# Neighbourhood layer: the low parts of all weights are made on VectorE, none on GpSimd

## The chip, the cores and the metric

The kernel runs on one core of a Trainium2 chip. The metric is the device time of one execution in microseconds (us), the median of three timed runs. Instructions run on five engines, which the trace calls PE (TensorE, with PEld for its weight loads), DVE (VectorE), ACT (ScalarE), POOL (GpSimd) and SP (SyncE, which here issues the DMAs).

## The reference, cut to what matters

Two layers of a diffusion backbone on 512 latent tokens (a grid of 8 rows by 64 columns) and 256 context tokens, 1024 features each. A layer normalises and modulates the tokens, projects them, mixes them, gates the result and projects it back. Layer 0 mixes with differential attention, layer 1 (the layer of the change) with attention over a neighbourhood on the grid, plus all context tokens:

```
def neighbourhood_mixer(u_lat, u_ctx, w_in, w_out, ...):
    q, k, v, z = jnp.split(u @ w_in, 4, axis=-1)      # latent and context tokens
    q = rms_norm(q per head of 64); k = rms_norm(k per head of 64)
    s     = q . k over an 8 x 16 window * scale + relative bias
    s_ctx = q . k_context * scale
    p     = softmax(concatenate([s, s_ctx]))
    o     = p_band . v_band + p_ctx . v_context
    return (o * silu(z)) @ w_out
```

All is float32. Layer 1 has 32 heads of 64 features; `w_in` is 1024 x 8192.

## The kernel before, in words

**Arithmetic.** The tensor engine takes operands in a reduced float32 format (float32r). To keep the accuracy, each operand x is held as two tiles: a high part, hi = float32r(x), and a low part, lo = x - hi. A product is three matmuls: hi hi, hi lo and lo hi (`project`, line 505). For weights, `split_w` (line 480) makes both: one DMA brings a raw tile `wraw` of two blocks of 128x512, ScalarE casts each block into `whi`, and then an engine subtracts, `wlo = wraw - whi`. That engine is VectorE unless the caller passes another.

**Loops.** Layer 1 runs over 16 groups of two heads. In the loop over groups (method `run`), step g does the attention of group g and, in the same ten half steps, the projections of group g + 1, as work that TensorE can do in between. The weights of a group come in four parts, q0 to q3, of two blocks each (eight blocks are the 1024 features in tiles of 128). `loads` (line 498) asks in step g for q0 at half step 6, q1 and q2 at half step 9, all for group g + 2, and for q3 at half step 0 for group g + 1. The tuple `POOL_B` names the parts whose low tiles are made by GpSimd: (0, 2), so q0 and q2; those of q1 and q3 are made by VectorE. That holds for groups 2 to 15; the weights of groups 0 and 1 are asked for outside `loads`, and their low parts are VectorE's. Layer 0 has the same scheme with `POOL_A`, which is empty: in its groups VectorE makes all low parts, apart from those of group 0.

**Buffers.** There are two `wraw` buffers, eleven `whi` and eleven `wlo` (`BUFS`, line 34). A raw buffer is free for the next DMA when both low tiles of its part are made. A `whi`/`wlo` buffer is free when TensorE has used its weights for the last of the six tiles of 128 tokens that a group projects.

**Other work on these engines.** In a group VectorE also normalises q and k (`qd`, `kk`), splits the transposed queries and keys (`qT`, `KSb`), the values (`Vb`) and the transposed softmax weights (`wTb`), adds the bias (`Sb`) and joins halves (`pair`). GpSimd finishes 1/rms (`ssk`, `rsk`) and multiplies by the gate (`yb`).

**Order.** Nothing is issued where it is noted. The class `Plan` (lines 131 to 277) notes every instruction and simulates a run: an engine takes, among the instructions that are ready at that moment, the one that was noted first. The order in which the simulated run starts them is the order in each engine's queue, which the chip then follows strictly. The simulation takes a price for each instruction (`Op.estimate`, line 94), among them

```
if e == "DVE": ...  return n / 0.96 + (129 if len(reads) > 2 else 69)     # ns; 602 for 128x512
if e == "POOL": ... return n * 0.83 + 36 if name == "memset" else n * 2.1 + 150   # 1225 for 128x512
```

It has no term for one engine's work slowing another's. In the profile all instructions carry line 277, where the plan issues them, so they are told apart by tiles.

Of the kernel before, what the change touches and what calls it, by code (L numbers as in the profile page):

```python
# [15 lines left out]
PSUM = bass.MemoryType.PSUM  # L16
DRAM = bass.MemoryType.DRAM
# [8 lines left out]
# token halves of 256: 0 = context, 1 and 2 = latent  # L26
# [10 lines left out]
# half steps of a projection between the parts of the attention  # L37
LAG = dict(pw=2.5, pv=1.5, po=0.5, py=1.5, qka=2, qkb=3, b1=2, b2=1.5, b3=1, bo=0.5, by=3)
# half steps at which the weights of the next groups are loaded, and the scores of a head begin
AT = dict(a0=8, a1=11, a2=11, a3=0, b0=6, b1=9, b2=9, b3=0, s0=5, s1=7, c0=2, c1=7, sa=0, cg=2, ch=9, c2=9, cv=1)  # L40
# half steps of the last group that begin an output projection
FILL_A, FILL_B = (0, 1, 2, 3, 5, 7, 9, 11, 13, 15, 16, 17), (2, 4, 6, 8, 10, 11, 12, 13)
START_DVE = (0,)
# parts of the first modulation that the tensor engine takes in float32
# [9 lines left out]
POOL_A, POOL_B = (), (0, 2)  # L54


class Pool:
    """tiles of a pool by tag, with the number of buffers of each tag in one place"""
# [12 lines left out]
# ns from the end of an instruction to the start of one that needs it  # L71
# [12 lines left out]
class Op:  # L84
    """an instruction that waits for its place: its engine, what it touches, what it is likely to take"""
# [8 lines left out]
    def estimate(self, name):  # L94
        """ns"""
        out, reads, e = self.writes[0], self.reads, self.engine
        n = math.prod(out.shape[1:])
        psum = any(x.space == PSUM for x in [out] + reads)
        if e == "PE":
            return 2.5 + n * (1 if reads[0].dtype == F32R else 2 if name == "transpose" else 4) / 2.4 if n > 2 else 260  # L100
        if e == "ACT":
            return n / 1.2 + (51 if psum else 93) + 93 * (len(self.writes) - 1 + name.startswith("act") * (len(reads) - 1))
        if e == "DVE":
            if name == "tensor_reduce":
                return math.prod(reads[0].shape[1:]) / 0.96 + 66
            if name in ("tensor_scalar", "tensor_copy", "memset") and not psum:
                return n / 1.92 + 69 + 60 * (len(reads) - 1)
            return n / 0.96 + (129 if len(reads) > 2 else 69)
        if e == "POOL":
            if any(x == ALU.pow for x in self.args):  # L110
                return 300 + 165 * n
            return n * 0.83 + 36 if name == "memset" else n * 2.1 + 150
        return max(56, math.prod(out.shape) / 90)


class Rec:
    """an engine that notes its instructions"""
# [13 lines left out]
class Plan:  # L131
    """notes the program, then issues every engine's instructions in the order of a simulated run"""
# [6 lines left out]
    def touching(self, tiles):  # L139
        """what has been noted so far that touches one of these"""  # L140
        names = {t.name for t in tiles}
        return {i for i, op in enumerate(self.ops) if any(x.name in names for x in op.writes + op.reads)}

    @staticmethod
    def region(x):
        """of a tile: partitions and columns, or all of it in PSUM; of memory in DRAM: the range"""
        dims = list(x.ap)
        if x.space == DRAM:
            return 0, 1, x.offset, x.offset + sum(s * (n - 1) for s, n in dims) + 1
        lo = x.offset % math.prod(x.tensor.shape[1:])  # L150
        hi = lo + 1 + sum(s * (n - 1) for s, n in dims[1:] if s > 0)
        lo += sum(s * (n - 1) for s, n in dims[1:] if s < 0)
        if x.space == PSUM:
            return 0, P, 0, 1
        p = x.start_partition
        p = p() if callable(p) else p
        return p, p + dims[0][1], lo, hi

    def depend(self):
        """what each instruction has to come after"""  # L160
        seen = {}
        for i, op in enumerate(self.ops):
            op.after = set(op.behind)
            at = [(x, self.region(x), w) for w, xs in ((True, op.writes), (False, op.reads)) for x in xs]
            for x, r, w in at:
                # two engines do not read a tile in PSUM at a time
# [14 lines left out]
    def order(self):  # L181
# [4 lines left out]
        place, count = {}, {}  # L186
# [16 lines left out]
        def offer(i):  # L203
            """to its engine, unless a buffer is missing"""
# [18 lines left out]
        out = []  # L223
        while len(out) < len(ops):
# [11 lines left out]
            # two of a tag at once, or a buffer gone since  # L236
# [4 lines left out]
            if e == "PE":  # L241
                # the tensor engine's clock is halved after an idle window
# [37 lines left out]
class K:  # L280
# [3 lines left out]
    # ------------------------------------------------------------ constants  # L284
# [19 lines left out]
    def load_vecs(self):  # L304
        """silu of both conditioning vectors, on every partition"""
# [23 lines left out]
    def mod_first(self):  # L329
        """scale and shift of layer 0 on the tensor engine; two steps per two tiles of features"""  # L330
# [7 lines left out]
        # columns: hi of both vectors, lo of both; their sums are the products with the weights' hi and lo  # L338
# [53 lines left out]
    def first_u(self, x, v, u, n, half):  # L392
        """two tiles of features of u hi / lo from x / rms"""
# [12 lines left out]
    def scaled(self, x, s, half):  # L406
        """x / rms, in place"""
        for n in range(4):
            eng = self.nc.gpsimd if 4 * half + n in X_POOL else self.nc.vector
            eng.tensor_tensor(x[n], x[n], s.unsqueeze(1).broadcast_to([P, 2, 256]), ALU.mult)  # L410

    def mod_chunk(self, layer, ch):
        """e[:, ch] = (W^T chunk) . silu(c) for both vectors"""
# [9 lines left out]
    def mod_finish(self, layer, v, part):  # L423
        """part 0: shift b, 1: a = g (1 + scale), 2: gate"""
# [8 lines left out]
    # ------------------------------------------------------------ modulated norm  # L433
    def norm_stats(self, x, tag="qd", on_pool=False):
        """x: four [128, 2, 256] (feature-major) -> 1 / rms, on every partition"""
# [9 lines left out]
        # a token to a partition for the power, then to every partition  # L445
# [14 lines left out]
    def make_u(self, x, s, a, b):  # L460
        """x, 1 / rms -> u hi / lo"""
# [17 lines left out]
    # ------------------------------------------------------------ weights  # L479
    def split_w(self, src, n, shape, eng=None, tag="wraw"):  # L480
        """n blocks of weights in one load, hi and lo each"""
# [16 lines left out]
    def loads(self, Wn, W, layer, g, hs, on_pool):  # L498
        """weights of the next groups: the last part of g + 1 and the others of g + 2"""
# [5 lines left out]
    def project(self, o, W, u, j, kts, c=slice(0, 512)):  # L505
        """one tile of 128 tokens (tile j of a half) x the columns of a group"""
# [10 lines left out]
    # ------------------------------------------------------------ order of work: half steps  # L517
# [3 lines left out]
    def tick(self, step=0.5):  # L521
        """everything that is due by now"""
# [9 lines left out]
    def drained(self, gen, fill, hs):  # L532
        """what is left of the attention, with the steps of other work for the half steps that follow"""
# [7 lines left out]
    # ------------------------------------------------------------ per-head rms of q and k  # L541
# [5 lines left out]
    def rstd(self, sq):  # L547
        """squares [128, 2, 128] -> 1 / rms of each 64 columns, [128, 4]"""
# [8 lines left out]
    def put_q(self, t, rs, dst):  # L557
        """t [128, 128] (two heads) times rs, each head twice, into dst [128, 2, 2, 64]"""
# [9 lines left out]
    def q_transposed(self, qds):  # L568
        """two tiles [128, 2, 2, 64] -> [128, head, hi / lo, 256]"""
# [15 lines left out]
    def k_transposed(self, ks, KS, half):  # L585
        """two tiles [128, 128] -> stacks of hi and lo; head 0: (hi; lo), head 1: (lo; hi)"""
# [16 lines left out]
    def gained(self, out, x, g):  # L603
        """[128, 2, 128] times a gain [128, 2, 64] of both heads"""
# [3 lines left out]
    def rope(self, ps, t):  # L608
        """(q | k) of a latent tile, rotated and times the norm's gains"""
# [14 lines left out]
    # ------------------------------------------------------------ layer 0: differential attention  # L624
    def a_tables(self):
# [16 lines left out]
        # (1 - lam_init) * gain of the sub-layer norm, with the half of the gate's silu  # L642
        nc.sync.dma_start(self.subg, A["subg"].broadcast_to([P, P]))
        nc.vector.tensor_scalar(self.subg, self.subg, 0.5 * (1.0 - LAM_INIT) * math.sqrt(P), None, ALU.mult)
        # -lambda
# [15 lines left out]
    def a_tile(self, G, half, j, ps):  # L661
        """queries, keys, values and gate of a tile of 128 tokens"""
# [37 lines left out]
    def a_scores(self, g, G, half, j):  # L700
        """scores of 128 queries with both heads' keys, softmax and difference of the two"""
# [20 lines left out]
        # l0 (p0 / l0 - lambda p1 / l1); the norm that follows takes l0 out again  # L722
# [67 lines left out]
    # ------------------------------------------------------------ layer 1: neighbourhood attention  # L790
    def b_tables(self):
# [3 lines left out]
        # the scores come out negated: q's gain carries the sign  # L795
# [12 lines left out]
    def b_project(self, G, U, W):  # L808
# [3 lines left out]
        for half in range(3):  # L812
            V = sb.tile([P, 2, 4, 64], F32R, name="Vb", tag="V")
            G["v"][half] = V
            if half == 0:
                # keys and values alone: both tiles share a bank
# [44 lines left out]
    def b_v_hi(self, ps, V):  # L861
        """values [.., 128] -> [.., 4, 64]: head 0: hi | lo, head 1: lo | hi"""
# [6 lines left out]
    def b_bias(self, g, h):  # L869
        """minus the bias, and what masks: one per place of a query block in the row; the last part is for the context"""  # L870
# [43 lines left out]
    def b_weights(self, pn, kts):  # L914
        """transposed weights of the key tiles asked for: 0..3 latent, 4 and 5 context"""
# [33 lines left out]
    def b_third(self, g, G, h, o, w):  # L949
        nc, pair = self.nc, G["pair"]  # L950
        self.b_values(G, h, o, w)
        # the halves of the products with the values' hi and lo
# [7 lines left out]
    def b_gate(self, g, G):  # L960
        nc, sb = self.nc, self.sb
        # silu carries a half
# [24 lines left out]
    # ------------------------------------------------------------ output projection  # L987
    def keep(self, layer, g, py, c):
        """what the last group leaves goes straight to an output projection that has begun"""
# [8 lines left out]
    def out_proj(self, layer, halves, gates, places, xtag, xs, late=None):  # L998
        """h + gate * (y @ w_out) of the tokens of one half or two; a step per 128 features, and one for the first loads;
        late: buffers for the rest of y, the last part first, for a second round"""  # L1000
# [77 lines left out]
    # ------------------------------------------------------------ everything  # L1078
# [168 lines left out]
def _host(inp):  # L1247
# [9 lines left out]
    # a head's 64 features as (half of the rotation, axis, frequency)  # L1257
# [31 lines left out]
    # relative bias: query p = (column, row), key (column offset, row)  # L1289
# [53 lines left out]
```

## Time and profile before

| | |
|---|---|
| time, median of 3 runs | 1829.35 us (1828.93 to 1829.58) |
| span of the profiled execution, first to last instruction | 1827.4 us |
| PE busy | 1775.6 us (97% of the span) |
| PEld busy | 1509.2 us (83%) |
| DVE busy | 1487.5 us (81%) |
| ACT busy | 969.8 us (53%) |
| POOL busy | 602.2 us (33%) |
| chain that ended last | PE 75%, DVE 15%, ACT 5% |

The span is what the trace shows of one execution; its own time on the clock of the timed runs is not recorded separately, and the median of those runs is 1.95 us above the span. The groups of layer 0 run from about 75 to 780 us and the groups of layer 1 from about 1050 us to 1690 us; output projections follow each.

A matmul's duration overlaps the next one's: 128x512 matmuls of 0.39 us start every 0.23 us. So PE counts as idle only where no matmul runs at all. Where a row of the timeline joins several instructions (x2, x3), its duration is from the first start to the last end.

### The profile page before, as it was taken

Reading aid. Unit: us, or ns where it says so; the run is one execution under the profiler, and the core shown is the slowest. Engines: PE = TensorE matmul, PEld = TensorE weight load, DVE = VectorE, ACT = ScalarE, POOL = GpSimd, SP = SyncE. Lnnn points to the kernel's source line nnn. Section 1 sums busy time; section 2 is a strip of 40 time slices with the busy share of each in tenths; the row PEclk is TensorE's granted clock in tenths of the full one; section 3 lists DMA queues with packets and bytes.
Section 4 is the critical chain, followed back from the end, with each engine's and each line's share of the span. In section 5 each row is a group of like instructions: output and inputs, shape, how many; then the busy total and the mean of one; then the engine's idle time right before and its main releaser. Section 6 shows DMA issues by size and latency. Waiting matters only on the chain.

```text
span 1827.4 us, 29430 instructions
## 1 busy us (share of the span) xinstructions
PE 1775.6 (97%) x10032; PEld 1509.2 (83%) x10032; DVE 1487.5 (81%) x3437; ACT 969.8 (53%) x2654; POOL 602.2 (33%) x915
## 2 busy tenths in 40 slices
PE   7899999999999999999999999999999999999999
PEld 3688888888888888888889988888888888888887
DVE  5888999898999999989858777777777777777863
ACT  4456555555555555556636455555555555555641
POOL 4544434444444444343100123333333333332100
PEclk9899999999999999999999999999999999999999
DMA  7401222121222222223556321111122211111423
GB/s 282 136 15 56 76 79 67 56 71 59 65 78 87 79 79 76 78 72 105 187 156 215 100 78 62 61 61 61 63 70 68 67 61 61 61 61 61 146 95 104
DMA packets 60774, 160.74 MB, mean 88 GB/s; under 512 B 7376, under 2 KB 22096, under 8 KB 59728
## 3 DMA queue, kind: packets, MB, share of 16 engines
q1 hardware_dynamic: 60624, 158.86, 26.7%
q8 instruction: 79, 1.29, 0.3%
q14 instruction: 71, 0.58, 0.1%
HBM read 144.68 MB, written 14.16 MB: 87 GB/s over the span
## 4 chain that ended last, share of the span: by engine, by line
PE 75%; DVE 15%; ACT 5%; issue 2%; POOL 2%; DMA 0%; SPq 0%; DVEq 0%; ACTq 0%; POOLq 0%
PE pj L277 40%; PE pjo L277 12%; PE oT L277 4%; PE S L277 4%; PE Sb L277 3%; PE pwb L277 3%; ACT pexp L277 3%; DVE wlo L277 3%; POOL ms L277 2%; PE pq L277 2%; DVE nm L277 2%; PE pw L277 1%; PE oTb L277 1%; DVE kk L277 1%; DVE t L277 1%
## 5 line engine op out<-in xcount | busy, mean ns | idle before, releaser
L277 PE MATMUL pj<-whi,ufirst 128*128 128x512 f32 x1536 | 524.6, 402 | 2.4 <-ACT ufirst L277 1.9
L277 PEld LDWEIGHTS pj<-whi,ufirst 128*128 128x128 f32 x1536 | 289.9, 189 | 58.1 <-ACT ufirst L277 2.5
L277 PE MATMUL pj<-wlo,ufirst 128*128 128x512 f32 x768 | 303.2, 395 | 0.0
L277 PE MATMUL pj<-wlo,uhi 128*128 128x512 f32 (+1 forms) x768 | 278.5, 363 | 12.1 <-DVE wlo L277 12.1
L277 PE MATMUL pj<-whi,uhi 128*128 128x512 f32 (+1 forms) x768 | 279.5, 364 | 0.0
L277 PE MATMUL pj<-whi,ulo 128*128 128x512 f32 (+1 forms) x768 | 276.3, 360 | 0.0
L277 ACT CAST whi<-wraw 128x512 fp32r<-128x512 f32 x352 | 209.3, 631 | 105.1 <-PE pjo L277 31.5
L277 DVE TENSOR_TENSOR wlo<-wraw,whi 128x512 fp32r<-128x512 f32 x288 | 220.6, 789 | 40.4 <-ACT whi L277 39.5
L277 POOL TENSOR_SCALAR ssk<-ssk 128x4 f32<-128x4 f32 x176 | 35.3, 201 | 556.9 <-DVE ssk L277 555.0
L277 ACT ACTIVATE pexp<-S,nm 128x768 f32<-128x768 f32 (+1 forms) x192 | 144.2, 758 | 127.8 <-DVE nm L277 127.7
L277 PE MATMUL pjo<-yhl,whi 128*128 128x512 f32 (+1 forms) x768 | 208.0, 357 | 0.0
L277 POOL TENSOR_TENSOR rsk<-ssk,mhalf 128x4 f32<-128x4 f32 x176 | 179.7, 1021 | 14.5
L277 PEld LDWEIGHTS pj<-wlo,uhi 128*128 128x128 f32 x768 | 145.2, 189 | 35.6 <-DVE wlo L277 19.0
L277 PEld LDWEIGHTS pj<-wlo,ufirst 128*128 128x128 f32 x768 | 145.8, 190 | 26.5
L277 PEld LDWEIGHTS pj<-whi,ulo 128*128 128x128 f32 x768 | 145.2, 189 | 17.9
L277 PEld LDWEIGHTS pj<-whi,uhi 128*128 128x128 f32 x768 | 145.3, 189 | 15.9
L277 PEld LDWEIGHTS pjo<-yhl,whi 128*128 128x128 f32 x768 | 134.8, 189 | 18.3
L277 DVE TENSOR_TENSOR wTb<-pwb,wTb 128x512 fp32r<-128x512 f32 (+2 forms) x192 | 101.1, 554 | 48.6 <-ACT wTb L277 47.7
L277 DVE TENSOR_REDUCE nm<-S 128x2 f32<-128x1536 f32 (+1 forms) x96 | 134.0, 1396 | 6.1 <-PE S L277 6.0
L277 PE MATMUL pjo<-yhl,wlo 128*128 128x512 f32 (+1 forms) x384 | 136.7, 356 | 0.0
L277 ACT CAST wTb<-pwb 128x512 fp32r<-128x512 f32 (+2 forms) x192 | 88.1, 487 | 88.8 <-PE pwb L277 87.2
L277 PE MATMUL S<-KS,qT 128*128 128x256 f32 (+1 forms) x640 | 132.8, 335 | 0.0
(161 smaller groups left out, 3552.5 us busy)
## 6 DMA issues: line engine op xcount, KB each, us to landing
wraw<-wa SPq DMA_DIRECT2D x64, 512.0 KB, 3.5
wraw<-wb SPq DMA_DIRECT2D x64, 512.0 KB, 3.9
modw<-modw SPq DMA_DIRECT2D x48, 512.0 KB, 3.8
wraw<-wo SPq DMA_DIRECT2D x24, 512.0 KB, 3.5
wraw<-wo SPq DMA_DIRECT2D x48, 256.0 KB, 3.2
yraw<-yd SPq DMA_DIRECT2D x14, 512.0 KB, 3.9
braw<-rpb SPq DMA_DIRECT2D x32, 192.0 KB, 2.4
yd<-yT SPq DMA_DIRECT2D x30, 128.0 KB, 1.9
```

The costliest lines, as they stand in the source:

```text
L277: op.f(*op.args, **op.kw)
```

## The change

One constant changes:

```
-POOL_A, POOL_B = (), (0, 2)
+POOL_A, POOL_B = (), ()
```

The rest of the diff takes comments and docstrings out. In `loads`, `on_pool` is now empty in layer 1 too, so that `split_w` gets no other engine and issues `nc.vector.tensor_tensor(lo, raw[:, i], hi, ALU.subtract)` for q0 and q2 of groups 2 to 15: 14 groups x 2 parts x 2 blocks = 56 instructions of 128x512 go from GpSimd to VectorE. The plan is made anew with VectorE's price for them, so that the order on every engine can differ from the first of the 56 on. The computation is the same.

## Rows read from the trace of the kernel before

**Rows 1.** Busy time of each engine by stretch: layer 0's groups, layer 1's groups.
```profile
core 0: us, PE busy (x) PEld busy (x) DVE busy (x) ACT busy (x) POOL busy (x), PEclk, DMA share, GB/s
75.00:780.00 705.00, 700.88 (x3831) 590.67 (x3829) 644.11 (x1554) 398.99 (x1229) 298.64 (x506) 1.00 0.23 70
1060.00:1670.00 610.00, 585.83 (x3513) 510.50 (x3512) 469.10 (x1095) 315.73 (x830) 191.14 (x248) 1.00 0.19 62
```
**Rows 2.** Waits of PE, 1060 to 1690: all in total, times, longest.
```profile
PE pj L277 <- DVE wlo L277: 12.1, 25, 0.6
PE pwb L277 <- DVE qT L277: 12.1, 14, 0.9
```
**Rows 3.** Timeline of PE, 1264 to 1279: start, duration, instruction, idle before.
```profile
1266.62 0.30 PE L277 MATMUL pwb<-ident,pb 128*128 128x128 f32 x1 [0.86 <-DVE qT L277]
...
1271.28 1.09 PE L277 MATMUL oTb<-wTb,Vb 128*128 128x384 f32 x6
...
1276.52 0.39 PE L277 MATMUL pj<-wlo,uhi 128*128 128x256 f32 x1 [0.36 <-DVE wlo L277]
...
1278.21 0.39 PE L277 MATMUL pj<-wlo,uhi 128*128 128x256 f32 x1 [0.62 <-DVE wlo L277]
```
**Rows 4.** Timeline of POOL, 1262 to 1279.
```profile
1264.15 2.66 POOL L277 TENSOR_TENSOR wlo<-wraw,whi 128x512 fp32r<-128x512 f32 x2 [0.23 <-ACT whi L277]
...
1274.62 2.98 POOL L277 TENSOR_TENSOR wlo<-wraw,whi 128x512 fp32r<-128x512 f32 x2 [0.58 <-ACT whi L277]
```
**Rows 5.** Timeline of DVE, 1264 to 1279.
```profile
1264.29 1.38 DVE L277 TENSOR_TENSOR kk<-t,rsk 128x128 f32<-128x128 f32 x1
...
1265.80 0.68 DVE L277 TENSOR_TENSOR qT<-pq,qT 128x512 fp32r<-128x512 f32 x1
1266.51 0.86 DVE L277 TENSOR_TENSOR KSb<-pk,KSb 64x256 fp32r<-64x256 f32 x2
1267.40 0.69 DVE L277 TENSOR_TENSOR wlo<-wraw,whi 128x512 fp32r<-128x512 f32 x1
1268.14 1.05 DVE L277 TENSOR_TENSOR wTb<-pwb,wTb 128x384 fp32r<-128x384 f32 x2
1269.90 0.42 DVE L277 TENSOR_TENSOR wTb<-pwb,wTb 128x256 fp32r<-128x256 f32 x1 [0.71 <-ACT wTb L277]
...
1271.65 0.69 DVE L277 TENSOR_TENSOR wTb<-pwb,wTb 128x512 fp32r<-128x512 f32 x1 [0.66 <-ACT wTb L277]
...
1274.82 3.33 DVE L277 TENSOR_TENSOR wlo<-wraw,whi 128x512 fp32r<-128x512 f32 x2
1278.08 0.67 DVE L277 TENSOR_TENSOR pair<-oTb,otmp 64x512 f32<-64x512 f32 x1
```
**Rows 6.** Tiles wlo and kk, 1060 to 1690: count, duration min/median/max in ns.
```profile
L277 POOL TENSOR_TENSOR wlo<-wraw,whi x56: 1292/1348/1828, 1060.5 to 1668.8; 128x512 fp32r<-128x512 f32 x56
L277 DVE TENSOR_TENSOR wlo<-wraw,whi x56: 681/693/1782, 1064.4 to 1678.7; 128x512 fp32r<-128x512 f32 x56
...
L277 DVE TENSOR_TENSOR kk<-t,rsk x84: 284/291/1390, 1065.1 to 1677.7; 128x128 f32<-128x128 f32 x84
```
**Rows 7.** Tiles rsk and wlo in layer 0's groups, 75 to 780.
```profile
L277 POOL TENSOR_TENSOR rsk<-ssk,mhalf x85: 1007/1015/1080, 86.6 to 777.3; 128x4 f32<-128x4 f32 x85
L277 DVE TENSOR_TENSOR wlo<-wraw,whi x110: 665/685/1000, 77.3 to 771.7; 128x512 fp32r<-128x512 f32 x110
```
**Rows 8.** Timeline of SP, the same stretch: DMA issues.
```profile
1268.12 0.80 SPq L277 DMA_DIRECT2D wraw<-wb  x2
```
**Rows 9.** DMA issues by line: count, size of one, median us to landing.
```profile
wraw<-wb SPq DMA_DIRECT2D x64, 512.0 KB, 3.9
```
**Rows 10.** Timeline of ACT, the same stretch: casts into whi.
```profile
1262.93 1.68 ACT L277 CAST whi<-wraw 128x512 fp32r<-128x512 f32 x3
```

## The prediction

> **What bounds the kernel now.** I read the busy time by stretch first. In layer 1's groups (610 us) PE is busy 585.83 us, so 24.2 us pass without a matmul; VectorE is at 77% (469.10 us) and GpSimd at 31% [rows 1]. TensorE sets the pace, and what can be won without taking matmuls out is those 24.2 us. The reader is to compare layer 0's row: there VectorE has 91% (644.11 of 705 us), and PE idles only 4.1 us [rows 1].
>
> Second, the list of waits, for PE alone. In layer 1 it has two entries: 12.1 us for `wlo` in 25 waits and 12.1 us for `qT` in 14 [rows 2]. Together 24.2 us, the whole of the idle time, so there is no third cause to look for.
>
> Third, the timeline of one group, to see why VectorE is late there. The groups repeat every 44.8 us. PE stops three times: 0.86 us before `pwb`, for `qT`, and 0.36 and 0.62 us for two `wlo` [rows 3], 1.84 us in all. The first stop: VectorE's `kk` took 1.38 us [rows 5] against a median of 0.29 [rows 6], while GpSimd made a `wlo` that had begun 0.14 us before it [rows 4]; `qT` comes behind `kk` in VectorE's queue. The other two: two `wlo` on VectorE took 3.33 us together [rows 5] against a median of 0.69 each [rows 6], beside two `wlo` on GpSimd from 1274.62 to 1277.60 [rows 4]. In both places an instruction of VectorE that reads two tiles of SBUF stood still while GpSimd subtracted. `qT`, which reads one of its two inputs from PSUM, took 0.68 us although GpSimd's second `wlo` ran on to 1266.81 beside it [rows 4, 5]. So all three stops stem from the 56 instructions that the change takes off GpSimd. These come as 28 pairs: one alone at 1060.5 us [rows 6], then 14 pairs like the one at 1264.15 and 13 like that at 1274.62.
>
> **The change part by part.**
>
> *What goes.* On GpSimd 56 x 1.35 us [rows 6]. On VectorE, per group, the stretching: `kk` 1.38 - 0.29 = 1.09 us, and the `wlo` pair 3.33 - 2 x 0.69 = 1.95 us; together 3.04 us [rows 5, 6].
>
> *What comes.* Four `wlo` per group on VectorE, 4 x 0.69 = 2.76 us [rows 6]. Net 0.28 us less per group, though it does more. Over the stretch: 469.1 + 56 x 0.69 - 14 x 1.09 - 13 x 1.95 = 467 us. So VectorE's load is no argument against the change; what counts is the places.
>
> *First place (q2).* The three casts at 1262.93 [rows 10] are q1's second block and both of q2: GpSimd begins when the second ends. VectorE makes q1's `wlo` at 1267.40 [rows 5] and would go on to q2's two. Without the stretch of `kk` it begins at 1267.40 - 1.09 = 1266.31 and is done with all three at 1266.31 + 3 x 0.69 = 1268.4. The next instruction, `wTb`, began at 1268.14: 0.3 us late. Behind it stand gaps of 0.71 and 0.66 us [rows 5], which swallow that; the three `wTb` before 1270.4 feed the `oTb` matmuls that begin at 1271.28 [rows 3], 0.9 us later. `kk`, `qT` and `KSb` belong to earlier half steps, are noted ahead of these `wlo`, and go first whenever they are ready. So `qT` comes 1.09 us earlier, and the stop of 0.86 us is gone with 0.2 to spare. If that cover fails, q2's two cost up to 1.38 us per group, 19 us in all.
>
> *Second place (q3 and q0).* The pair at 1274.82 is q3's, for the projection that runs at that moment. Unstretched it ends at 1275.5 and 1276.2. PE has work until 1276.52 - 0.36 = 1276.16 and, between the first and the second, for 1278.21 - 0.62 - 1276.52 = 1.07 us more, until 1277.2 [rows 3]: both are ready in time. q0's two are noted six half steps after q3's and come behind; all four end at 1277.6, before the 1278.08 at which `pair` begins now [rows 5]. q0's weights are wanted a group later.
>
> *DMA.* A raw buffer now comes free when VectorE is done. q3's load and q0's are issued at 1268.12 [rows 8], when q1's `wlo` ends; q3's moves ahead by up to 1.09 us. q0's waits for q2's, 1266.81 on GpSimd before and 1268.4 after: 0.3 us behind its issue now, which nothing waits for. SP issues in order, and q3's stands first.
>
> [...] In layer 0, where VectorE makes these tiles, GpSimd's `rsk` takes 1.015 us, at most 1.080 in 85, and VectorE's `wlo` 0.685, at most 1.000 in 110 [rows 7]. [...]
>
> *Sum.* 24.2 us of stops go [rows 2]. What comes back I bound from both sides: nothing at the least, and at the most all of it and more (the last rival). A new plan with VectorE at 79% (467 of about 590 us) will not be without any stop. The nearest row is layer 0's, 4.1 us in 705 at 91% [rows 1], so 3.6 us in 610, and I take that: 24.2 - 3.6 = 20.6 us saved. [...] The span goes from 1827.4 to 1806.8 us. The median of the timed runs lies 1.95 us above the profiled span, which makes 1808.7 us.
>
> **The rivals.**
>
> *One kind of stop stays (0.15).* A `wlo` that has begun is not interrupted. If the plan begins q2's two just ahead of `qT`, 1.38 us take the place of the 1.09 of `kk`: the stop for `qT` grows by 0.29, only the 12.1 us of the other kind go, and 12.1 - 14 x 0.29 = 8 us are saved, 1821 us. If q0's come before q3's, the second kind stays: 12.1 us saved, 1817 us. For it: from 1274.82 on VectorE has no gap [rows 5]. Against it: the plan knows the 0.60 us that it counts for a `wlo` and lays TensorE's work around it; of the stretching it knew nothing.
>
> *The contention turns round (0.05).* If one `rsk` per group is held up for a whole `wlo`, 0.69 us, and PE waits for all of it, 14 x 0.69 = 9.7 us come back: saved 24.2 - 3.6 - 9.7 = 10.9, 1818 us. Against it [rows 7].
>
> *No difference (0.08).* GpSimd keeps `rsk` and `yb`, so VectorE could go on being stretched by those and the edit not do what it says, or the new plan has stops as long as the old ones: 1826 to 1833 us. For it only that the sum of VectorE's work hardly changes; against it that PE's waits are laid to `wlo` and `qT` alone [rows 2].
>
> *Slower: q3's load comes late (0.12).* There are two raw buffers, and q3's load needs q1's. q1's `wlo` is noted after the `wTb` of the same moments. If it slips behind them, q3's load slips too: 3.9 us to landing [rows 9], two casts of about 0.6 [rows 10], the second block's `wlo` 0.69 [rows 6] and some 0.2 to PE, 6.0 us in all. PE wants that block at 1277.2, so the issue may be as late as 1271.2, 3.1 us after now, before PE stops for it; from 1271.2 + 1.84 = 1273.0 on the group is slower than before. Behind the last `wTb` before q3's own pair, at about 1274.0, it would cost 1.0 us per group more than now, 14 us, 1843 us. Against it: where q1's `wlo` stands now, the plan has VectorE without earlier work, and q2's are noted after q1's, so they can't push it back.
>
> **How the numbers follow.** The forecast has 0.60, with a range of its own from 1805 (nothing comes back) to 1815 us. About 0.2% of the time, 3.7 us, is what a measurement of this kernel can tell from no change. Faster: 0.60 + 0.15 + 0.05 = 0.80; same 0.08; slower 0.12. The range takes in the forecast and the rivals on its side up to the edge of no change, 1804 to 1826 us.
>
> **What would show it.** In the profile after: no `wlo` on POOL from 1060 us on, 112 on DVE with none far above 0.7 us; no `kk` of 1.38 us behind a `wlo` of GpSimd; PE's waits in layer 1 down from 24.2 to below 5 us; a period of about 43.2 instead of 44.8 us; VectorE near 79%. Wrong would be: an entry of more than 10 us in PE's waits there, above all for `wlo` with ScalarE's `whi` waiting for the DMA of `wraw`, or a wait of `qd` for `rsk` that has grown.

## The result, and the profile after

The changed kernel takes 1796.38 us (median of 4 runs, 1795.71 to 1798.46) against 1829.46 for the kernel before on the same chip: ratio 0.9819, 95% interval 0.9805 to 0.9833. That is 33 us saved, where 20.6 were forecast, and below the range of 1804 to 1826. The direction and the place were right, the size was not. The profiled spans are 1794.0 and 1827.4 us, a difference of 33.4.

Busy time by stretch (PE, PEld, DVE, ACT, POOL; then the granted clock, DMA share and GB/s), the answer to [rows 1]:

```profile
75.00:780.00 705.00, 701.37 (x3831) 590.88 (x3830) 644.76 (x1556) 398.50 (x1234) 295.49 (x508) 1.00 0.22 70
1060.00:1640.00 580.00, 580.00 (x3523) 509.87 (x3522) 463.19 (x1153) 318.56 (x834) 112.02 (x192) 1.00 0.21 65
```

Layer 0 is as it was. In layer 1 PE is busy without a gap, 580.00 of 580 us, and VectorE is at 80%. The list of PE's waits from 1060 to 1690 us, which had two entries [rows 2], is empty. The tiles `wlo` and `kk` there (count, ns min/median/max), against [rows 6]:

```profile
L277 DVE TENSOR_TENSOR wlo<-wraw,whi x120: 640/683/694, 1059.7 to 1688.5; 128x512 fp32r<-128x512 f32 x120
```

```profile
L277 DVE TENSOR_TENSOR kk<-t,rsk x86: 279/285/858, 1064.0 to 1658.0; 128x128 f32<-128x128 f32 x86
```

There is none on GpSimd, and none is stretched: the longest `wlo` on VectorE was 1.782 us and is 0.694. (The count is 120 and not 112, since the window now reaches 33 us further into the output projection.) The longest `kk` now, 0.858 us, stands beside `yb`, which GpSimd keeps. VectorE's timeline at the first place, against [rows 5]:

```profile
1254.20 0.28 DVE L277 TENSOR_TENSOR kk<-t,rsk 128x128 f32<-128x128 f32 x1
1254.41 0.28 DVE L277 TENSOR_TENSOR Vb<-pj,Vb 128x128 fp32r<-128x128 f32 x1
1254.61 0.68 DVE L277 TENSOR_TENSOR qT<-pq,qT 128x512 fp32r<-128x512 f32 x1
1255.32 0.86 DVE L277 TENSOR_TENSOR KSb<-pk,KSb 64x256 fp32r<-64x256 f32 x2
1256.21 1.29 DVE L277 TENSOR_TENSOR wlo<-wraw,whi 128x512 fp32r<-128x512 f32 x2
1257.53 1.02 DVE L277 TENSOR_TENSOR wTb<-pwb,wTb 128x384 fp32r<-128x384 f32 x2
1258.47 0.68 DVE L277 TENSOR_TENSOR wlo<-wraw,whi 128x512 fp32r<-128x512 f32 x1
1259.08 0.42 DVE L277 TENSOR_TENSOR wTb<-pwb,wTb 128x256 fp32r<-128x256 f32 x1
```

`kk` takes 0.28 us and `qT` follows at once. But the three `wlo` (q1's second, q2's two) are not in one run: the plan put the third behind two `wTb`. PE's timeline at both places, against [rows 3]:

```profile
1254.37 1.31 PE L277 MATMUL oTb<-wTb,Vb 128*128 128x512 f32 x6
1255.51 0.27 PE L277 MATMUL pwb<-ident,pb 128*128 128x128 f32 x1
...
1264.83 0.27 PE L277 MATMUL pwb<-ident,pb 128*128 128x128 f32 x1
1264.86 0.36 PE L277 MATMUL pj<-wlo,uhi 128*128 128x256 f32 x1
...
1265.43 0.36 PE L277 MATMUL pj<-wlo,uhi 128*128 128x256 f32 x1
```

The gaps are gone. Note the starts: `pwb` begins 1.14 us after the first of the six `oTb`, though their record lasts 1.31. That is the key to the size, below. The period, the time from one group to the next, is read from the chain of work that ended last, at the same run of 26 matmuls in two groups one after the other. Before:

```profile
1241.46 5.93 PE pj L277 x26
...
1286.24 5.93 PE pj L277 x26
```

After:

```profile
1231.36 5.95 PE pj L277 x26
...
1273.67 5.95 PE pj L277 x26
```

44.78 us became 42.31: 2.47 us a group, although the idle time of a group was 1.84. Over the span: the `pyb` transposes begin 2.65 us earlier in the first of 16 groups and 33.40 us earlier in the last, and nothing comes after.

### The profile page after: what moved, and what is told of

Its sections match the earlier page's. It is cut to its first block, busy times and chain, and to the rows that moved or that the text cites. A ratio compares the mean times of both kernels' runs of the same rounds, so it can differ in the third digit from the quotient of the medians.

```text
span 1794.0 us, 29417 instructions
## 1 busy us (share of the span) xinstructions
PE 1766.6 (98%) x10032; PEld 1506.1 (84%) x10032; DVE 1480.4 (83%) x3493; ACT 970.6 (54%) x2654; POOL 517.8 (29%) x859
## 3 DMA queue, kind: packets, MB, share of 16 engines
q8 instruction: 79, 1.29, 0.3%
## 4 chain that ended last, share of the span: by engine, by line
PE 85%; DVE 7%; ACT 4%; POOL 2%; issue 1%; DMA 1%; SPq 0%; DVEq 0%; ACTq 0%
PE pj L277 46%; PE pjo L277 12%; PE S L277 5%; PE oT L277 4%; PE oTb L277 4%; PE pwb L277 4%; PE Sb L277 3%; ACT pexp L277 2%; PE pq L277 2%; POOL ms L277 2%; PE pw L277 2%; PE pk L277 1%; DVE nm L277 1%; DVE y L277 1%; PE py L277 1%
## 5 line engine op out<-in xcount | busy, mean ns | idle before, releaser
L277 DVE TENSOR_TENSOR wlo<-wraw,whi 128x512 fp32r<-128x512 f32 x344 | 230.5, 696 | 31.6 <-ACT whi L277 30.7
L277 PEld LDWEIGHTS pj<-wlo,uhi 128*128 128x128 f32 x768 | 145.2, 189 | 16.6
L277 ACT ACTIVATE sqk<-pj 128x256 f32<-128x256 f32 x176 | 67.5, 384 | 124.3 <-PE pj L277 119.8
```

Source lines behind the costliest of these rows:

```text
L277: op.f(*op.args, **op.kw)
```

## The experiments

**Contention or order?** Theory A: VectorE's standstill beside GpSimd caused the stops. Rival B: the new order of all instructions brings the gain. The first two runs keep one and undo the other: in `split_w`, the engine that executes an instruction is swapped after the plan has it.

```
 # the changed kernel's plan; q0 and q2 of layer 1's loop:
             (eng or nc.vector).tensor_tensor(lo, raw[:, i], hi, ALU.subtract)
+            if self.swap:
+                nc.ops[-1].f = self.tc.nc.gpsimd.tensor_tensor
```

> The plan is that of the changed kernel, but the 56 instructions run on GpSimd. If VectorE's standstill beside GpSimd is the cause (theory A), VectorE's instructions with two SBUF inputs are stretched beyond 1 us again wherever they fall beside a wlo of GpSimd, PE stops again, and the time goes up by at least 12 us, to 1808 to 1830 us. If the gain came from the new order of the instructions (rival B), the time stays at 1794 to 1800 us.

Measured: 1831.99 us, ratio 1.001 (1.0001 to 1.0019). PE's waits in layer 1 (all in total, times, longest) and VectorE's `kk` and `wlo`:

```profile
PE pj L277 <- DVE wlo L277: 14.1, 25, 0.8
PE pwb L277 <- DVE qT L277: 12.1, 14, 0.9
```

```profile
L277 DVE TENSOR_TENSOR kk<-t,rsk x84: 278/290/1387, 1063.7 to 1678.2; 128x128 f32<-128x128 f32 x84
...
L277 DVE TENSOR_TENSOR wlo<-wraw,whi x56: 676/693/1773, 1063.0 to 1679.2; 128x512 fp32r<-128x512 f32 x56
```

With GpSimd back, all is back: the order alone gains nothing. The time is even 2 us above the range expected, as one wait for `wlo` in a group is longer than before (0.8 us, 0.6 before). The reverse, with the plan of the kernel before:

```
 # POOL_B = (0, 2), so that the plan is the one before
+            if self.swap:
+                nc.ops[-1].f = self.tc.nc.vector.tensor_tensor
```

> The plan is that of the kernel before, with GpSimd's price and place for the 56 instructions, but they run on VectorE. Theory A: no kk above 1.1 us, no wlo above 1.0 us, the three stops of a group gone, 1796 to 1806 us (some new stops, as VectorE's order was not made for it). Rival B: the old order keeps the loss, 1822 to 1832 us.

Measured: 1811.79 us, ratio 0.9899 (0.9886 to 0.9913). Between the theories: no `wlo` is stretched (0.694 us the longest) and no `kk` beyond 0.86, and all three stops are gone, but one new one stands in every group in the list. PE's waits, then VectorE's and PE's timelines there:

```profile
PE pwb L277 <- DVE wTb L277: 10.6, 14, 0.8
```

```profile
1260.36 1.90 DVE L277 TENSOR_TENSOR wlo<-wraw,whi 128x512 fp32r<-128x512 f32 x3
1262.29 1.02 DVE L277 TENSOR_TENSOR wTb<-pwb,wTb 128x384 fp32r<-128x384 f32 x2
```

```profile
1258.52 1.31 PE L277 MATMUL oTb<-wTb,Vb 128*128 128x512 f32 x6
...
1261.76 0.39 PE L277 MATMUL pj<-whi,uhi 128*128 128x512 f32 x1
1262.90 0.33 PE L277 MATMUL pwb<-ident,pp 128*128 128x128 f32 x1 [0.75 <-DVE wTb L277]
```

Three `wlo` in a row hold up `wTb`, and the next transposes `pwb` wait for it: they need the PSUM buffer that `wTb` reads out. So the end of the contention is worth 18.7 us without a new plan. TensorE's order is the same, instruction for instruction, as in the kernel before, so that the distance from one matmul's start to the next can be compared at every place: where the kernel before stopped, 32.9 us are gone, and 15.5 us are new at two `pwb` of each group, this one (0.92 us later) and a later one (0.20 us, hardly visible as idle time). That makes 17.4 us; about 1 us more lies before 75 us, where both kernels do the same. Is the rest the place of that third `wlo` alone? In the same kernel it is issued two places later on VectorE; the orders of TensorE and SyncE stay.

```
...
+            # q2's second wlo behind the next two of VectorE, in the finished order
+            out[a : b + 1] = stay + moved
```

> As the run with the old order on VectorE (1811.8 us, which has one new stop a group, 0.75 us before pwb for wTb, behind three wlo in a row), but the third of these three is issued two places later on VectorE, behind the two wTb; TensorE's and SyncE's order stay as they were before the change. If that place is all that the new plan adds to the end of the contention, the stop shrinks below 0.2 us a group and the time falls to 1796 to 1801 us. If the new plan's other changes (TensorE's order) are needed, it stays at 1808 to 1812 us.

Measured: 1803.85 us, ratio 0.9855 (0.9838 to 0.9871): 8 of the 15 us that were missing, between the two expectations. What is left of PE's waits (this file is longer, its line is 291):

```profile
PE pwb L291 <- DVE wTb L291: 1.7, 11, 0.2
```

The period is 42.83 us, 0.52 above the changed kernel's, and the waits show 0.15 of that. From start to start two places of the period are late, 0.32 us ahead of `pwb` for `wTb` and 0.20 us at a later `pwb`. Over all groups these two places make 7.2 us. So the place of that `wlo` is half of the 15 us, and the other 7 lie at these two `pwb`. Which of the new plan's other moves clears them, TensorE's order or VectorE's, was not shown: no run changes TensorE's order alone.

**Which part makes which stop?** One of the two parts on VectorE at a time, the plan made for it.

```
-POOL_A, POOL_B = (), ()
+POOL_A, POOL_B = (), (2,)      # and (0,) in the other run
```

> Only q0 goes to VectorE; q2 stays on GpSimd. Theory A: kk of 1.38 us and the stop for qT stay, the two stops for q3's wlo go. A stop priced by the extra time from one matmul's start to the next (1.45 us a group for these two, 13 groups): 18.9 us saved against the kernel before, 1810.5 us. Priced by the idle time that the waits show (0.98 us a group): 12.7 us saved, 1816.7 us. Rival B (a new plan as such): no fixed share, 1796 or 1829 us as likely.

Measured: 1809.3 us, ratio 0.9887 (0.9872 to 0.9902), 21.1 us saved. The stop for `qT` stays, as it was; the others are gone:

```profile
PE pwb L277 <- DVE qT L277: 12.1, 14, 0.9
```

> Only q2 goes to VectorE; q0 stays on GpSimd. Theory A: the stop for qT goes, the two for q3's wlo stay, with a wlo pair of 3 us or more on VectorE. Start to start 1.02 us a group, 14 groups: 14.3 us saved, 1815.1 us. By the idle time of 0.86 us: 12.0 us saved, 1817.4 us. With the other half the savings should add up to the whole, 33 us, if the stops are independent.

Measured: 1817.32 us, ratio 0.993 (0.9917 to 0.9942), 13.1 us saved; the stop for `qT` is gone, the other kind stays:

```profile
PE pj L277 <- DVE wlo L277: 12.3, 22, 0.8
```

The halves add up: 1.13% and 0.70% make 1.83%, the whole is 1.81%. Of the two prices in the expectations, the first run speaks for the one from start to start. The second lies near the price by idle time, but the stops left in it are other ones than before: one wait of about 0.5 us in some groups, two of 0.3 and 0.8 in others. Their periods, 43.1 and 44.0 us, are 0.8 and 1.7 us above the changed kernel's 42.31, more than the 0.5 and 1.1 us of idle time; this speaks for start to start too.

**Does reading or any work of GpSimd stretch VectorE's instructions?** Rival C: GpSimd's results came late, and the stretching is a side effect. The changed kernel gets work on GpSimd that nobody waits for, counted by the plan at nothing (PE's order is the changed kernel's, instruction for instruction).

```
...
+                nc.scalar.copy(scr[:, i, 0:1], hi[:, 0:1])     # starts it
+                for _ in range(2):
+                    nc.gpsimd.tensor_tensor(scr[:, i], hi[:, 0:256], hi[:, 256:512], ALU.subtract)
```

> The changed kernel, every wlo made on VectorE in its order, plus work on GpSimd that nobody waits for: behind each whi of q2 and q0 two subtractions of 128x256 that read that whi twice (about 0.75 us each), and a one-column copy on ScalarE that starts them. If VectorE stands still because GpSimd reads SBUF at that time (theory A), kk and wlo are stretched beyond 1 us, PE stops again for qT and wlo, 1808 to 1832 us. If the loss came from the results of GpSimd being late, or from its queue (rival C), the time stays at 1794 to 1800 us, as nobody needs these results.

Measured: 1821.21 us, ratio 0.9946 (0.9931 to 0.9961). VectorE's `wlo`, the first place on GpSimd and on VectorE, and the longest of PE's four entries:

```profile
L277 DVE TENSOR_TENSOR wlo<-wraw,whi x112: 670/797/1270, 1061.2 to 1670.6; 128x512 fp32r<-128x512 f32 x112
```

```profile
1263.14 3.39 POOL L277 TENSOR_TENSOR scr<-whi 128x256 bf16<-128x256 f32 x4 [0.86 <-ACT scr L277]
```

```profile
1264.66 2.42 DVE L277 TENSOR_TENSOR wlo<-wraw,whi 128x512 fp32r<-128x512 f32 x2
```

```profile
PE pwb L277 <- DVE wTb L277: 14.4, 14, 1.0
```

Rival C falls: PE's waits are for VectorE (16.6 us), apart from one of 0.3 us for `scr`. One thing in the expectation was wrong: the extra work begins after `kk` (the longest `kk` is 0.854 us), so the stop is not for `qT` but for the `wTb` behind two stretched `wlo`. GpSimd's subtractions of 128x256 suffer too: at least 0.725 us, median 0.942, longest 1.596. The same with writing alone:

```
-                for _ in range(2):
-                    nc.gpsimd.tensor_tensor(scr[:, i], hi[:, 0:256], hi[:, 256:512], ALU.subtract)
+                for _ in range(5):
+                    nc.gpsimd.memset(scr[:, i], 0.0)
```

> As the run with the extra subtractions, with the same start, but the extra work only writes: five memsets of 128x256 behind each of these whi (0.31 us each, 1.56 us together). [...]

Measured: 1798.0 us, ratio 0.9821 (0.9806 to 0.9835), the changed kernel's. GpSimd's timeline at the first place, VectorE's beside it, and all `wlo`:

```profile
1257.28 2.82 POOL L277 MEMSET scr<- 128x256 bf16 x10 [0.82 <-ACT scr L277]
```

```profile
1258.84 1.29 DVE L277 TENSOR_TENSOR wlo<-wraw,whi 128x512 fp32r<-128x512 f32 x2
```

```profile
L277 DVE TENSOR_TENSOR wlo<-wraw,whi x119: 637/684/695, 1059.9 to 1687.7; 128x512 fp32r<-128x512 f32 x119
```

Two `wlo` run beside 2.82 us of GpSimd's memsets and take 1.29 us, as without; beside GpSimd's subtractions two took 2.42 us. So of the two kinds of extra work the subtractions, which read SBUF, stretch `wlo`, and the memsets, which only write, do not. On VectorE's side `qT` and `KSb`, which read one input from PSUM, kept their length beside the extra subtractions that run from 1263.14 to 1266.53 us: `qT` took 0.68 us there (0.675 to 0.682 in the changed kernel) and two `KSb` 0.86 us, as in the changed kernel. Beside GpSimd's `wlo` in the kernel before, `qT` took 0.675 to 0.677 us in 14 groups.

**What does a stop cost?** Here VectorE is held up by work of its own ahead of `qT`, so that only the delay is tested. In the first run this work stands behind `kk`:

```
+            nc.vector.tensor_tensor(scr, b, b, ALU.subtract)     # x2, b = ks[1], planned at nothing
```

> The price of a stop without GpSimd. The changed kernel, with two subtractions of 128x256 on VectorE (0.35 us apart) ahead of each qT of the first latent half, which the plan counts at nothing, so that the order is that of the changed kernel. qT comes 0.7 us later, with slack of about 0.1 us, so the next matmul starts about 0.6 us late in 14 or 15 groups. If a stop costs the delay from start to start, 14 x 0.6 = 8.4 us, 1804.8 us, with about 0.45 us of idle time shown for each. If it costs the idle time that the waits show, 6.3 us, 1802.7 us.

Measured: 1799.09 us, ratio 0.9827 (0.9812 to 0.9841). The two subtractions landed ahead of a group of `wTb`, where VectorE had slack, and not ahead of the `qT` that PE waits for. The period is 42.42 us, 0.11 longer. Two more runs hang the extra work on the cast of `qT` itself:

```
         nc.scalar.copy(qT[:, 0], pq)
+        for i in range(late):                                    # late = 1, or 2 in the other run
...
+            nc.vector.tensor_tensor(scr, qT[:, 0], qT[:, 0], ALU.subtract)
```

> The price of a stop without GpSimd, at the place where the kernel before had its stop for qT. The changed kernel, with one subtraction of 128x512 on VectorE (nobody needs it, the plan counts it at nothing, TensorE's order is unchanged) just ahead of the qT that pwb waits for. qT comes about 0.6 us late; with slack of about 0.1 us the next matmul starts some 0.5 us late. If the period of a group (42.30 us) grows by the delay from start to start, it comes to 42.8 us, 15 groups x 0.5 = 7.5 us more than the changed kernel, 1804 us, and the waits show 0.16 us less than that a group (a matmul's record outlasts its place by 0.16 us), about 0.35. If it grows by the idle time shown alone, 1801.5 us. If such a stop costs nothing, since other work makes up for it, 1796 to 1798 us.

Measured: 1806.48 us, ratio 0.9874 (0.9858 to 0.9891). Period 42.92 us, 0.61 more than the changed kernel's. PE's timeline at the stop:

```profile
1257.19 1.30 PE L277 MATMUL oTb<-wTb,Vb 128*128 128x512 f32 x6
1258.87 0.30 PE L277 MATMUL pwb<-ident,pb 128*128 128x128 f32 x1 [0.37 <-DVE qT L277]
```

> The same with two subtractions, so that qT comes about 1.2 us late, as kk's standstill of 1.09 us made it in the kernel before. Start to start 1.1 us a group: period 43.4 us, 15 x 1.1 = 16.5 us more than the changed kernel, 1813 us, with about 0.95 us a group shown as a wait for qT. By the idle time alone 1810.5 us. A second stop, for wTb, may appear, as everything behind on VectorE is late too: then up to 0.5 us a group more.

Measured: 1820.69 us, ratio 0.9946 (0.9931 to 0.996). Period 43.65 us, 1.34 more.

```profile
1264.01 1.30 PE L277 MATMUL oTb<-wTb,Vb 128*128 128x512 f32 x6
1266.42 0.30 PE L277 MATMUL pwb<-ident,pb 128*128 128x128 f32 x1 [1.11 <-DVE qT L277]
```

From the first `oTb` to `pwb` it is 1.68 and 2.41 us, 1.14 in the changed kernel: 0.54 and 1.27 us more, where the waits show 0.37 and 1.11. Both times the wait is 0.16 to 0.17 short. That is what a matmul's record outlasts its place: 128x512 is recorded for 0.39 us and the next starts after 0.23. TensorE's order is the same in all three kernels, so that every start can be set against the changed kernel's: in the 14 groups of the list the `pwb` behind `qT` come 7.8 and 17.8 us late, where the waits show 5.6 and 15.6; with the 15th group, behind the list's window, it is 8.3 and 19.1 us. The profiled spans grew by 10.2 and 25.0 us. Of the rest of the 25.0, 2.7 us lie before 75 us, where the two kernels do the same, and 1.5 us at two other late matmuls of layer 1; 1.7 us are spread over the span. Both times exceed what either price forecast (1806.5 against 1804, 1820.7 against 1813), since `qT` came later than assumed and these other places were not counted. At every one of these stops the price by idle time is too low.

The run with the new order on GpSimd shows the same for the stops of this case. Its order on TensorE is the changed kernel's too. Against the changed kernel's starts the 25 matmuls that waited for `wlo` come 20.2 us late and the 14 that waited for `qT` 14.3, together 34.5 us; the list shows 26.2, and the spans differ by 33.8.

## Why the prediction was wrong, by its own steps

*Who is late, and why: right.* All three stops came from VectorE's standstill beside GpSimd's `wlo`, and each went with its part. The load was right as well: 467 us forecast for VectorE in about 590, 463.19 in 580 measured. `rsk` was not held up: its mean in layer 1 was 1.022 us and is 1.020, and PE has no wait behind it. q3's load delayed nothing. The queues kept the plan's order: in the traces before and after, SyncE's 421 DMA issues stand in it, and so do VectorE's 3437 and 3493 instructions.

*"What can be won without taking matmuls out is those 24.2 us": wrong, the step that failed.* A stop was priced at the idle time of the waits, but the engine was also short of matmuls while the last one's record still ran. The kernel before and the run with the old order on VectorE have the same order on TensorE, so their starts can be set side by side. Before, beside [rows 3]:

```profile
1264.47 1.30 PE L277 MATMUL oTb<-wTb,Vb 128*128 128x512 f32 x6
...
1275.88 0.27 PE L277 MATMUL pwb<-ident,pb 128*128 128x128 f32 x1
...
1277.11 0.48 PE L277 MATMUL pj<-whi,uhi 128*128 128x512 f32 x1
...
1278.43 0.28 PE L277 MATMUL pj<-whi,ulo 128*128 128x256 f32 x1
```

The old order on VectorE, at the second and third stop:

```profile
1269.84 0.27 PE L277 MATMUL pwb<-ident,pb 128*128 128x128 f32 x1
1269.87 0.36 PE L277 MATMUL pj<-wlo,uhi 128*128 128x256 f32 x1
...
1270.44 0.48 PE L277 MATMUL pj<-whi,uhi 128*128 128x512 f32 x1
1270.76 0.28 PE L277 MATMUL pj<-wlo,uhi 128*128 128x256 f32 x1
1270.87 0.28 PE L277 MATMUL pj<-whi,ulo 128*128 128x256 f32 x1
```

The first stop is 2.15 us from the first `oTb` to `pwb`, where 1.14 is the distance without it: 1.01 us. The second is 0.64 against 0.03, so 0.61 us. The third is 1.10 against 0.32, and the matmul behind it has 0.22 against 0.11, so 0.89 us. Together they are 2.51 us, not 1.84, and the period fell by 2.47. Over all groups the term of 24.2 us measured 32.9. So 1805 us, where nothing comes back, was no lower bound, and the range that began at 1804 missed.

*"What comes back": 3.6 us taken, nothing measured with the plan made anew.* Layer 0's 4.1 us of idle time was the wrong neighbour: its list of waits names 1.9 us, 1.3 of them for `y`. With both terms right the sum nearly closes: 20.6 + 3.6 + 8.7 = 32.9 of the 33.4 us by which the span fell.

*"First place": the outcome right, the working wrong.* I laid three `wlo` in one run, let the `wTb` behind them be 0.3 us late, and looked only to the `oTb` that read them. I measured this against the old timeline, but TensorE, without its stop, comes to this place 1.0 us earlier. The run with the old order has exactly this: its first `wTb` begins 3.77 us after the first `oTb`, where it was 3.67 before, and `pwb` waits 0.75 us for the PSUM buffer that `wTb` empties. The gaps did not swallow it. That the stop was gone in the changed kernel was, for this part of the working, luck. What saved the step is the plan: it knew the 0.60 us that it counts for each, put the third one behind two `wTb`, and laid TensorE's order anew. That is 15 us of the gain (1811.79 against 1796.38), of which 8 come back by moving that one instruction. So the 33 us have two conditions: the contention must go (without that the new order is worth nothing) and the order must be made for the new owner.

*The rivals.* "One kind of stop stays" did not happen with the plan made anew, but it is what the run with the old order shows, with `wTb` in the place of `qT`. Of "no difference" a part is true: `yb` on GpSimd still stretches one `kk` in a group to about 0.85 us (0.847 to 0.858), as it did before (0.844 to 0.858), but no matmul waits for it. The others did not show. The 0.69 us for which "the contention turns round" has an `rsk` held up stands in neither trace, before or after: the longest `rsk` in layer 1 was 1.070 us before and is 1.069, with medians of 1.010 and 1.007. That a begun `wlo` is not interrupted holds in both traces: VectorE's next instruction began at the earliest 0.09 us before the end of one (288 and 344 of them).

## What to carry to other kernels

Price a stop of TensorE from one matmul's start to the next against the usual distance; the idle time in the list of waits left out 0.15 to 0.27 us of each stop here, and nearly all of those of 0.20 us. When one instruction takes several times its median, look at what the neighbouring engine ran beside it: moving that work onto the "busier" engine can make this engine less busy (here VectorE's busy time over the execution fell from 1487.5 to 1480.4 us, with 56 more instructions). And when work changes its owner, let the order be made anew: here 15 of 33 us hung on the order, and 8 of them on one instruction's place in a queue.

## What the runs showed of the hardware that was not expected

In the run with the extra memsets VectorE's `wlo`, a subtraction of two SBUF tiles, lost nothing beside 2.82 us of GpSimd's memsets (0.684 us median, 0.695 longest; 0.683 and 0.694 in the changed kernel). In the run with the extra subtractions, which read SBUF, `wlo` lost up to 0.6 us (1.270 longest, 0.670 shortest), and GpSimd's subtractions lost up to 0.87 us in return (1.596 against 0.725). The 0.20 us by which a `pwb` of the swapped run was late appears in no list of waits, since the record of the matmul before it covered almost all of it.
